# First layer's norm: adaLN weights in groups of 256 channels, each chunk normed, modulated and multiplied as its group arrives

## The chip, the cores and the metric

One core of a Trainium2 chip runs the whole kernel. The metric is device time in microseconds (us). Engines are named as in the profile: PE (TensorE, matrix products), PEld (its weight loads), DVE (VectorE), ACT (ScalarE), POOL (GpSimd), SP (SyncE, which issues most of the DMA transfers).

## The reference, cut to what matters

Two layers run one after the other on a residual stream x of 1024 tokens by 1024 channels. Each layer norms and modulates its input, projects it to 5912 columns, runs two attention mixers and adds a gated output projection:

```
mod = silu(c) @ ada_w + ada_b                 # c: 1024 values; ada_w: 1024 x 3072 per layer
shift, scale, gate = split(mod, 3)
h = rms_norm(x, norm_g) * (1 + scale) + shift
proj = h @ w_in                               # 1024 x 5912
a = stick_breaking_attention(sb_q, sb_k, sb_v) * silu(sb_z)
b = native_sparse_attention(rope(rms_norm(n_q)), ...) * silu(n_z)
y = sigmoid(m_a) * (a @ w_proj_a) + sigmoid(m_b) * (b @ w_proj_b)
x = x + gate * (y @ w_out)
```

All is float32. The change touches the first three lines, and the first product of the fourth, in layer 0 alone.

## The kernel before

A float32 product runs as three passes: each operand is split into a high part (rounded on ACT, `hi`) and a low part (difference on DVE, `lo`), and hi*hi, hi*lo and lo*hi are summed in PSUM. Channels are handled in 8 chunks of 128, tokens in 2 halves of 512. The normed input is held transposed, channels on partitions, so that scale and shift are one number per partition: `A = norm_g * (1 + scale)` and `B = shift`, as [128, 8] columns.

The function `norm_first` is the start of the kernel. PE, DVE and ACT run its instructions in the order in which it writes them (`manual_schedule`, L326); what later functions emit is placed between them by the planner of the framework. SP issues loads in the order written, and a load into a buffer that is still in use makes SP, and all loads behind it, wait.

In order, `norm_first` does this:

- SP loads four x tiles (first half, 512 KB each, L465), the identity (L519) and three small vectors (c, ada_b, norm_g; L341 to L343), then the scale part of ada_w as 8 tiles [128, 1024] through 5 buffers (L472), three raw weight tiles of the first projection group (L175), the shift part of ada_w in the same way, the fourth raw tile and the four x tiles of the second half. The rope tables, the masks and the next group's weights follow.
- ACT squares the x tiles (L488). DVE turns the vectors into columns (L347) and makes silu(c) (L350).
- `rsqrt` takes three Newton steps on a [128, 4] tile: start value on DVE (L146 to L148), 12 steps on POOL (L152 to L155), since `on_pool` is set here. ACT then scales the x tiles (L529), PE transposes them (L436), and ACT copies all 8 transposed chunks out of PSUM (L532).
- DVE sums the scale part over the 8 tiles, `acc = acc + ada * silu(c)_k` (L478, L481); PE multiplies each 128-column slice of `acc` with a column of ones (L373), which sums over partitions; DVE makes A (L540, L541). The shift part goes the same way and gives B in two halves of 4 chunks (L546).
- `chunks(0, ...)`: for each chunk `modulate` makes `h = x*A + B` and its high part on ACT (L444, L445, even chunks) or h on DVE and the high part on ACT (L447, L448, odd chunks), then the low part on DVE (L449); then 6 products per chunk (L496), for two column groups of 128 by three passes. Between them, on ACT and DVE, lie squares (L488, L490), Newton steps and scaling of the second half, and the splits of the weight tiles (L136, L137).
- `chunks(1, ...)` does the same for the second half, with the transposes (L436) between the products and the rope tables (L635) on DVE. The low part of a chunk is taken after the next chunk's first step.

The results of the first half lie in two PSUM buffers (`proj`), those of the second in two others (`sc`). Then `early` goes on with the other projection groups (lines L194, L196, L198 in the profile); they need the split weights and a `proj` buffer.

Of the kernel before, what the change touches and what calls it, by code (L numbers as in the profile page):

```python
# [37 lines left out]
def make_consts():  # L38
    """Constants that depend on shapes alone, packed along the free dimension of 128 partitions."""
# [48 lines left out]
class Trunk:  # L88
    def __init__(self, tc, I, O, depth=2, dbg=None):
# [7 lines left out]
        # amount of projection work that is put between the bursts of an attention job, by query pair  # L97
# [5 lines left out]
        # how far dependent transposes are put off  # L103
# [9 lines left out]
        self.adb = 5  # L113

    # ---------------------------------------------------------------- helpers
# [23 lines left out]
    def rsqrt(self, pool, ss, n, inv, tag, on_pool=False):  # L139
        """1/sqrt(ss * inv + EPS) by Newton steps; ss [rows, n]."""  # L140
# [9 lines left out]
        for _ in range(3):  # L150
            if on_pool:
                nc.gpsimd.tensor_tensor(t, y, y, ALU.mult)  # L152
                nc.gpsimd.tensor_tensor(t, t, v, ALU.mult)
                nc.gpsimd.tensor_scalar(t, t, -0.5, 1.5, ALU.mult, ALU.add)
                nc.gpsimd.tensor_tensor(y, y, t, ALU.mult)  # L155
            else:
                nc.vector.tensor_tensor(t, y, y, ALU.mult)
                nc.vector.scalar_tensor_tensor(t, t, -0.5, v, ALU.mult, ALU.mult)
                nc.vector.scalar_tensor_tensor(y, t, 1.5, y, ALU.add, ALU.mult)
# [18 lines left out]
    def split_raw(self, raw):  # L178
        """Tile [128, hi/lo, 2, columns]."""
        n = raw.shape[2]  # L180
        w = self.tl(self.wpool, [P, 2, 2, 280], F32R, "w", bufs=self.wb)
        self.split(raw, w[:, 0, :, :n], w[:, 1, :, :n])
        return w

    def load_group(self, srcs, ncols):
        """The four tiles of a weight group."""
        return [self.split_raw(raw) for raw in self.load_raw(srcs, ncols)]

    def mm3_gen(self, ps, pairs, cost):
        """Three-pass product over pairs ((lhs_hi, lhs_lo), (rhs_hi, rhs_lo)), matmul by matmul."""  # L190
# [21 lines left out]
    def t_unit(self, w, u, half, act, ks=range(KD)):  # L212
        """[128 columns, 512 tokens] = w columns^T @ act^T for one half of the tokens."""
# [4 lines left out]
    def n_unit(self, w, t, act, ncols):  # L218
        """[128 tokens, ncols] = act tokens @ w."""
# [4 lines left out]
    def n_units(self, w, ts, act, ncols):  # L224
        """n_unit of several token tiles, the last chunk of the contraction after the others of all."""
# [16 lines left out]
    def defer(self, us, f):  # L242
        """Emit f once us of tensor-engine work have gone by, so that its operands are ready."""
# [58 lines left out]
    # ---------------------------------------------------------------- start  # L302
# [30 lines left out]
    # ---------------------------------------------------------------- adaLN modulation  # L333
    def vectors(self, pool, l):
        """Biases of the modulation [128, shift/scale, 8] and norm gain [128, 8] of layer l, model dimension on
        partitions; the first layer's call also makes silu(c)."""
        nc, I = self.nc, self.I
        n = 32 if l == 0 else 24
        rows = self.tl(pool, [n, P], F32, "vrows")
        if l == 0:  # L340
            nc.sync.dma_start(rows[24:32], I["c"].rearrange("o (k p) -> (o k) p", p=P))  # L341
        nc.sync.dma_start(rows[0:16], I["ada_b"][l, 0:2 * D].rearrange("(k p) -> k p", p=P))
        nc.sync.dma_start(rows[16:24], I["norm_g"][l].rearrange("(k p) -> k p", p=P))  # L343
# [9 lines left out]
    def mod_part(self, pool, l, part, sc, tag, steps):  # L353
        """acc[p, j] = sum over chunks k of ada_w[k*128+p, part*1024 + j] * silu(c)[k*128+p], one step per chunk."""
# [45 lines left out]
    def mod_gate(self, l, pool, steps):  # L400
        """The residual gate on every partition; returns it and the part that uses the tensor engine."""
# [13 lines left out]
    # ---------------------------------------------------------------- norm  # L415
# [4 lines left out]
    def norm_rows(self, pool, xs, tag, on_pool=False):  # L420
        """x * rsqrt(mean(x^2) + eps), in place, of the [128, 1024] tiles xs."""
# [6 lines left out]
        r = self.rsqrt(pool, ss, n, 1.0 / D, tag, on_pool)  # L428
# [3 lines left out]
    def norm_t(self, xs, k):  # L432
        """PSUM [128 channels of chunk k, 512 tokens]."""
# [5 lines left out]
    def modulate(self, pool, src, a, b, hi, lo, bufs=2, on_scalar=False):  # L439
        """src * a + b, split; returns the last step."""  # L440
# [10 lines left out]
    def norm_first(self):  # L451
        """Norm of the input, and the first product on it, in the order in which the loads arrive."""
        tc, nc, I = self.tc, self.nc, self.I
        rope = self.open_rope(0)
        with tc.tile_pool(name="norm0", bufs=1, reuse_waits="tile") as pool:
            A = self.tl(self.lay, [P, KD], F32, "Acol", bufs=2)
            B = self.tl(self.lay, [P, KD], F32, "Bcol", bufs=2)
            ada = {}
            acc = [self.tl(pool, [P, D], F32, f"acc{part}") for part in range(2)]

            def load_x(half):
                xs = []
                for t in range(4):
                    x = self.tl(pool, [P, D], F32, "x", bufs=4)
# [4 lines left out]
            def load_ada(part):  # L469
                for k in range(KD):  # L470
                    a = self.tl(pool, [P, D], F32, "ada", bufs=self.adb)
# [981 lines left out]
```

## Time and profile before

| | |
|---|---|
| median of 3 runs | 2231.28 us (2230.01 to 2231.57) |
| span of the profiled execution | 2229.4 us |
| PE busy | 2131.1 us, 96% |
| DVE busy | 1572.0 us, 71% |
| ACT busy | 1129.2 us, 51% |
| POOL busy | 60.2 us, 3% |
| mean granted PE clock | 0.992 |

The execution's own time is its span from first to last instruction; the runs' times hold a little more around it. A granted clock of 1.00 is 2.4 GHz, 0.50 is 1.2 GHz. Busy shares are averages over the whole kernel; a stretch is read from the tables by stretch, and a chain of waits shows which wait ended last.

### The profile page before, as it was taken

What the parts mean: (1) busy time and instruction counts of PE and PEld (TensorE: products, weight loads), DVE (VectorE), ACT (ScalarE), POOL (GpSimd) and SP (SyncE); (2) the same over time, 40 slices, a digit from 0 to 9 for tenths busy, and PEclk for the clock granted to TensorE, in tenths of its full rate; (3) what the DMA queues carried; (4) which work ended last, traced back from release to release, by engine and by line L of the source; (5) the groups of instructions that cost most, each with busy time, mean ns of one, the idle gap of its engine ahead of it and who ended that gap; (6) DMA issues with size and microseconds to landing.
All of it is one profiled execution on the core that took longest, in us unless ns stands there. A gap on an engine that the chain in (4) does not pass through costs nothing.

```text
span 2229.4 us, 36753 instructions
## 1 busy us (share of the span) xinstructions
PE 2131.1 (96%) x13128; PEld 1841.4 (83%) x13128; DVE 1572.0 (71%) x3714; ACT 1129.2 (51%) x2481; POOL 60.2 (3%) x226
## 2 busy tenths in 40 slices
PE   3999999999999999999999998999999999999999
PEld 3899778988887777789889986889898877777899
DVE  5857558868765877877765852887788487787643
ACT  4533147656665655663443421665666465656410
POOL 2100000000000000000010000000000000001000
PEclk8999999999999999999999999999999999999999
DMA  7435862252116445275455355322522364534433
GB/s 286 131 124 180 250 156 79 88 151 96 66 49 165 127 125 137 86 246 174 159 149 160 97 189 141 94 86 86 142 91 67 92 154 112 149 100 168 150 123 102
DMA packets 239256, 297.04 MB, mean 133 GB/s; under 512 B 21993, under 2 KB 186721, under 8 KB 239073
## 3 DMA queue, kind: packets, MB, share of 16 engines
q1 hardware_dynamic: 198560, 250.65, 36.6%
q10 hardware_dynamic: 36224, 29.37, 5.1%
q0 software_dynamic: 4288, 14.68, 2.0%
q8 instruction: 103, 1.69, 0.3%
q14 instruction: 81, 0.66, 0.1%
HBM read 206.28 MB, written 83.89 MB: 130 GB/s over the span
## 4 chain that ended last, share of the span: by engine, by line
PE 66%; DVE 17%; DMA 7%; issue 5%; ACT 3%; POOL 1%; SPq 0%; ACTq 0%; DVEq 0%; POOLq 0%
PE proj L194 15%; PE proj L198 15%; PE proj L196 15%; PE tr L879 6%; DVE C L1243 4%; PE av L899 4%; PE av L898 3%; PE sc L866 3%; PE sc L867 3%; DVE wl L137 2%; DVE E L1244 2%; DMA ada<-in_ada_w 2%; DVE w L137 2%; DMA kk<-QK 1%; DMA q<-QK 1%
## 5 line engine op out<-in xcount | busy, mean ns | idle before, releaser
L194 PE MATMUL proj<-acthi,w 128*128 128x512 f32 x1312 | 536.9, 409 | 1.3 <-ACT acthi L136 0.7
L196 PE MATMUL proj<-actlo,w 128*128 128x512 f32 x1312 | 536.8, 409 | 0.5 <-DVE actlo L137 0.5
L198 PE MATMUL proj<-acthi,w 128*128 128x512 f32 x1312 | 536.2, 409 | 0.7 <-DVE w L137 0.7
L136 ACT CAST w<-raw 128x512 fp32r<-128x512 f32 (+1 forms) x296 | 183.4, 622 | 230.1 <-PE proj L198 119.0
L137 DVE TENSOR_TENSOR wl<-tr,wh 128x512 fp32r<-128x512 f32 (+2 forms) x432 | 256.6, 610 | 40.8 <-ACT wh L136 38.4
L194 PEld LDWEIGHTS proj<-acthi,w 128*128 128x128 f32 x1312 | 249.4, 190 | 42.1 <-ACT acthi L136 1.6
L196 PEld LDWEIGHTS proj<-actlo,w 128*128 128x128 f32 x1312 | 249.4, 190 | 39.0 <-DVE actlo L137 1.9
L198 PEld LDWEIGHTS proj<-acthi,w 128*128 128x128 f32 x1312 | 249.0, 190 | 37.9 <-DVE w L137 1.2
L137 DVE TENSOR_TENSOR w<-raw,w 128x512 fp32r<-128x512 f32 (+1 forms) x296 | 202.2, 688 | 81.9 <-ACT w L136 79.8
L136 ACT CAST wh<-tr 128x512 fp32r<-128x512 f32 (+2 forms) x432 | 221.2, 527 | 76.1 <-PE tr L879 70.7
L899 PE MATMUL av<-wl,V 128*128 128x256 f32 (+1 forms) x864 | 217.5, 285 | 7.6 <-DVE wl L137 7.3
L194 PE MATMUL proj<-w,acthi 128*128 128x256 f32 (+1 forms) x768 | 221.2, 288 | 2.2 <-DVE s L137 1.7
L198 PE MATMUL proj<-w,actlo 128*128 128x256 f32 (+1 forms) x768 | 221.0, 288 | 0.0
L196 PE MATMUL proj<-w,acthi 128*128 128x256 f32 (+1 forms) x768 | 219.8, 286 | 0.0
L898 PE MATMUL av<-wh,V 128*128 128x256 f32 (+1 forms) x864 | 216.8, 271 | 1.2 <-DVE o L917 0.5
L879 PE MATMUL tr<-ident,E 128*128 128x128 f32 x1152 | 187.3, 276 | 23.7 <-DVE E L1244 23.0
L1243 DVE TENSOR_TENSOR_SCAN C<-C 128x128 f32<-128x128 f32 (+7 forms) x128 | 172.5, 1349 | 53.0 <-ACT C L1239 52.4
L879 PEld LDWEIGHTS tr<-ident,E 128*128 128x128 f32 x1152 | 139.2, 140 | 67.4 <-DVE E L1244 35.0
L899 PEld LDWEIGHTS av<-wl,V 128*128 128x128 f32 x864 | 162.7, 188 | 31.1 <-DVE wl L137 19.3
L866 PE MATMUL sc<-kk,q 128*128 128x512 f32 (+3 forms) x512 | 176.8, 346 | 8.6 <-DVE mx L1079 4.1
L867 PE MATMUL sc<-kk,q 128*128 128x512 f32 (+3 forms) x512 | 175.5, 343 | 0.0
L898 PEld LDWEIGHTS av<-wh,V 128*128 128x128 f32 x864 | 163.0, 189 | 14.0 <-ACT wh L136 3.9
(247 smaller groups left out, 3898.2 us busy)
## 6 DMA issues: line engine op xcount, KB each, us to landing
raw<-in_w_in SPq DMA_DIRECT2D x168, 256.0 KB, 2.9
ada<-in_ada_w SPq DMA_DIRECT2D x48, 512.0 KB, 5.3
kk<-QK SPq DMA_DIRECT2D x48, 512.0 KB, 9.0
q<-QK ACTq DMA_DIRECT2D x64, 256.0 KB, 4.0
QK<-s SPq DMA_DIRECT2D x32, 512.0 KB, 3.0
MD<-sz SPq DMA_DIRECT2D x64, 256.0 KB, 2.6
QK<-s SPq DMA_DIRECT2D x48, 256.0 KB, 3.3
VD<-s SPq DMA_DIRECT2D x48, 256.0 KB, 2.1
```

The source lines that it names most:

```text
L136: nc.scalar.copy(hi, src)
L137: nc.vector.tensor_tensor(lo, src, hi.bitcast(F32), ALU.subtract)
L194: nc.tensor.matmul(ps, lh, rh, start=(x == 0), stop=False)
L196: nc.tensor.matmul(ps, lh, rl, start=False, stop=False)
L198: nc.tensor.matmul(ps, ll, rh, start=False, stop=(x == n - 1))
L866: nc.tensor.matmul(ps, q, k[:, 0, c0:c1], start=True, stop=False)
L867: nc.tensor.matmul(ps, q, k[:, 1, c0:c1], start=False, stop=not masks)
L879: nc.tensor.transpose(pt[:, x * P:x * P + P], b, self.ident)
L898: nc.tensor.matmul(ps[:, c:d], lhsT, hi[:, a:b], start=(first and x == 0), stop=False, skip_group_check=True)
L899: nc.tensor.matmul(ps[:, c:d], lhsT, lo[:, a:b], start=False, stop=(last and x == n - 1), skip_group_check=True)
L1243: nc.vector.tensor_tensor_scan(rev, rev, rev, 1.0, ALU.mult, ALU.bypass)
L1244: nc.vector.tensor_tensor(e[:, 0:nk], e[:, 0:nk], c[:, 1:nk + 1], ALU.mult)
```

## The change

`rsqrt` loses `on_pool`; all its steps run on DVE (3 per Newton step instead of 4). The identity and the three small vectors are issued by ACT instead of SP. ada_w's scale and shift parts come in 4 groups of 256 channels each, one tile [128, 8, 256] per part and group, by two DMAs of 512 KB whose rows are 1 KB; three such buffers serve both parts. The x tiles have 8 buffers instead of 4.

The scale part of a group is now summed on PE: 8 accumulating products of a 128 x 128 block with a column of silu(c), for each of 2 chunks. The shift part is summed on DVE over 256 columns and then over partitions on PE. The copies of the transposed chunks are gone; `modulate` reads PSUM. All 8 chunks of the first half use the form with h and high part on ACT, and the low part is taken at once, in both halves. Squares, Newton steps and scaling of the second half follow the last chunk of the first half; squares alternate between ACT and DVE, and so does scaling, in both halves.

The core of the diff (old `load_ada`, `add`, `chunks` and the old sequence are removed):

```diff
-            if on_pool:
-                nc.gpsimd.tensor_tensor(t, y, y, ALU.mult)
-                ...
-            else:
-                nc.vector.tensor_tensor(t, y, y, ALU.mult)
+            nc.vector.tensor_tensor(t, y, y, ALU.mult)
...
+            def load_ada(part, g):
+                a = self.tl(pool, [P, KD, W], F32, "ada", bufs=3)
+                src = I["ada_w"][0, :, part * D + g * W:part * D + g * W + W].rearrange("(k p) n -> p k n", p=P)
+                for k in range(0, KD, 4):
+                    nc.sync.dma_start(a[:, k:k + 4], src[:, k:k + 4])
+                return a
...
+            def scale_cols(g):
+                a = ada[1, g]
+                pt = self.tl(self.pav, [P, 512], F32, "av", bufs=1)
+                for j in range(2):
+                    for k in range(KD):
+                        nc.tensor.matmul(pt[:, j:j + 1], a[:, k, j * P:j * P + P], sc[:, k:k + 1],
+                                         start=(k == 0), stop=(k == KD - 1))
+                return pt
+            def shift_acc(g):
+                a = ada[0, g]
+                acc = self.tl(pool, [P, W], F32, "acc", bufs=2)
+                nc.vector.tensor_scalar(acc, a[:, 0], sc[:, 0:1], None, ALU.mult)
+                for k in range(1, KD):
+                    nc.vector.scalar_tensor_tensor(acc, a[:, k], sc[:, k:k + 1], acc, ALU.mult, ALU.add)
+                return acc
+            def shift_cols(acc):      # two products of acc with ones, in a "tr" buffer of PSUM
...
+            xs = [load_x(0)]
+            ab, gn = self.vectors(pool, 0, nc.scalar)
...
+            for part in (1, 0):
+                ada[part, 0] = load_ada(part, 0)
+            gen = self.plan.pop(0)()
+            raws = [next(gen) for _ in range(2)]
             for t in range(4):
+                square(0, t, t % 2 == 0)
+            r = self.rsqrt(pool, ss[0], 4, 1.0 / D, "nr0")
+            for t in range(4):
+                scale(0, t, r)
+            w = [self.split_raw(raws[0])]
+            for g in range(1, G):
+                for part in (1, 0):
+                    ada[part, g] = load_ada(part, g)
+                if g < 3:
+                    raws.append(next(gen))
             xs.append(load_x(1))
+            tr = [self.norm_t(xs[0], 0), self.norm_t(xs[0], 1)]
+            pa = scale_cols(0)
+            fin_a(0, pa)
+            fin_b(0, shift_cols(shift_acc(0)))
+            for g in range(G):
+                k = 2 * g
+                mod(0, k, tr.pop(0), True)
+                if g + 1 < G:
+                    pa = scale_cols(g + 1)
+                mm(0, k)
+                mod(0, k + 1, tr.pop(0), True)
+                if g + 1 < G:
+                    tr.append(self.norm_t(xs[0], k + 2))
+                    w.append(self.split_raw(raws[g + 1]))
+                    fin_a(g + 1, pa)
+                    acc = shift_acc(g + 1)
+                mm(0, k + 1)
+                if g + 1 < G:
+                    tr.append(self.norm_t(xs[0], k + 3))
+                    fin_b(g + 1, shift_cols(acc))
+            for t in range(4):
+                square(1, t, t % 2 == 0)
+            r = self.rsqrt(pool, ss[1], 4, 1.0 / D, "nr1")
+            for t in range(4):
+                scale(1, t, r)
             tables = rope()
             next(tables)
+            for k in range(KD):
+                mod(1, k, self.norm_t(xs[1], k), k % 2 == 0)
+                if k:
+                    mm(1, k - 1)
+                next(tables, None)
+            mm(1, KD - 1)
```

## Rows read from the trace of the kernel before

**Rows 1.** The page's second part, 40 equal slices: PE's busy tenths.
```profile
PE   3999999999999999999999998999999999999999
```
**Rows 2.** Stretches: bounds, length, busy us (instructions) per engine, granted clock, DMA share, GB/s.
```profile
33.00:42.00 9.00, 1.67 (x15) 1.59 (x15) 7.11 (x9) 1.70 (x4) 0.00 (x0) 0.65 0.53 187
46.00:56.00 10.00, 8.96 (x19) 6.24 (x20) 8.80 (x19) 9.20 (x15) 1.55 (x4) 0.50 0.53 155
56.00:63.00 7.00, 6.86 (x29) 5.22 (x28) 4.66 (x11) 4.39 (x7) 2.04 (x9) 0.99 0.00 0
84.00:110.00 26.00, 26.00 (x211) 25.57 (x210) 24.57 (x106) 10.44 (x25) 4.27 (x8) 1.00 0.81 228
291.50:295.00 3.50, 3.50 (x17) 3.49 (x18) 0.64 (x4) 0.00 (x0) 0.00 (x0) 0.52 1.11 350
```
**Rows 3.** Chain that ended last, first 80 us: start, us, what.
```profile
3.94 6.27 DMA vrows<-in_norm_g
...
12.65 1.17 POOL nr0t L152
...
22.82 4.28 ACT x L529 x4
27.14 5.85 PE tr L436 x29
...
44.25 0.17 DVE Bcol L546
```
**Rows 4.** Groups by line and shape, first 110 us: busy, mean ns; idle before.
```profile
L481 DVE SCALAR_TENSOR_TENSOR acc<-ada,silu_c,acc 128x1024 f32<-128x1024 f32 x12 | 15.4, 1284 | 0.9 <-DMA ada<-in_ada_w 0.6
L449 DVE TENSOR_TENSOR actlo<-h,acthi 128x512 fp32r<-128x512 f32 x16 | 10.8, 682 | 0.0
L445 ACT CAST acthi<-h 128x512 fp32r<-128x512 f32 x8 | 5.0, 620 | 0.3
L444 ACT ACTIVATE h<-xt,Bcol,Acol 128x512 f32<-128x512 f32 x4 | 3.2, 809 | 10.5 <-DVE Bcol L546 9.8 <-DVE actlo L449 0.7
L481 DVE SCALAR_TENSOR_TENSOR acc<-ada,silu_c,acc 128x512 f32<-128x512 f32 x4 | 2.8, 750 | 0.7 <-DMA ada<-in_ada_w 0.7
L490 DVE CUSTOM_DVE_ANT_0 junk<-x 128x1024 bf16<-128x1024 f32 x2 | 2.4, 1217 | 0.0
```
**Rows 5.** Instructions in order of time: start, us, engine, line, operation.
```profile
9.54 1.06 ACT L488 ACTIVATE junk<-x 128x1024 bf16<-128x1024 f32 x1 [0.15 <-DMA x<-in_x]
...
53.55 0.17 DVE L146 TENSOR_SCALAR nr1v<-ss 128x4 f32<-128x4 f32 x1
53.75 0.17 DVE L147 TENSOR_SCALAR nr1i<-nr1v 128x4 int32<-128x4 int32 x1
...
63.26 1.03 PE L436 MATMUL tr<-ident,x 128*128 128x128 f32 x8
```
**Rows 6.** Instructions in order of time: products of one column on PE.
```profile
32.83 1.84 PE L373 MATMUL av<-ones,acc 128*128 128x1 f32 x16
...
42.38 1.84 PE L373 MATMUL tr<-ones,acc 128*128 128x1 f32 x8 [7.70 <-DVE acc L481]
...
289.65 5.00 PE L373 MATMUL proj<-ones,acc 128*128 128x1 f32 x32
```
**Rows 7.** Instructions in order of time: products of the first half.
```profile
51.35 1.05 PE L496 MATMUL proj<-acthi,w 128*128 128x512 f32 x2
...
52.63 1.05 PE L496 MATMUL proj<-acthi,w 128*128 128x512 f32 x2
```
**Rows 8.** Stretches, columns as in rows 2, with loads of 1 KB rows.
```profile
17.00:19.00 2.00, 0.00 (x0) 0.00 (x0) 1.96 (x2) 0.00 (x0) 1.92 (x2) 1.00 0.79 221
...
998.00:1000.00 2.00, 1.94 (x16) 1.97 (x17) 1.81 (x3) 0.31 (x1) 0.00 (x0) 1.00 0.96 315
```
**Rows 9.** Line 669, 80 to 95 us: POOL's copies into xs; landing holds SP's too.
```profile
L669 POOL DMA_DIRECT2D xs<-s x8: 598/598/808, 83.1 to 92.9; - x8
...
DMA to landing us min/median/max: 2.4/4.1/5.5
```

More of the change, by code (lines that the diff above doesn't have):

```diff
@@ L331, in run, with vectors @@
                 xsrc = dst
-    def vectors(self, pool, l):
+    def vectors(self, pool, l, eng=None):
         nc, I = self.nc, self.I
+        eng = eng or nc.sync
         n = 32 if l == 0 else 24
@@ L457, in norm_first @@
             B = self.tl(self.lay, [P, KD], F32, "Bcol", bufs=2)
-            ada = {}
-            acc = [self.tl(pool, [P, D], F32, f"acc{part}") for part in range(2)]
+            warm = self.tl(pool, [P, 1], F32, "warm")
+            nc.scalar.activation(warm, self.ones[:, 0:1], AF.Sigmoid)
+            nc.scalar.dma_start(self.ident, I["consts"][:, 0:P])
             def load_x(half):
@@ L467, in load_x, with square @@
                 return xs
-            def load_ada(part):
-                for k in range(KD):
-                    a = self.tl(pool, [P, D], F32, "ada", bufs=self.adb)
-                    nc.sync.dma_start(a, I["ada_w"][0, k * P:(k + 1) * P, part * D:part * D + D])
-                    ada[part, k] = a
-            def add(part, k0, k1):
-                for k in range(k0, k1):
-                    if k == 0:
-                        nc.vector.tensor_scalar(acc[part], ada[part, k], sc[:, 0:1], None, ALU.mult)
-                        continue
-                    for c in (slice(0, 512), slice(512, 1024)) if k == KD - 1 else (slice(0, 1024),):
-                        nc.vector.scalar_tensor_tensor(acc[part][:, c], ada[part, k][:, c], sc[:, k:k + 1],
-                                                       acc[part][:, c], ALU.mult, ALU.add)
-            def square(half, t, on_scalar=True):
+            def load_ada(part, g):
[4 more added lines that the diff above has]
+                return a
+            def square(half, t, on_scalar):
                 junk = self.tl(pool, [P, D], BF16, "junk")
@@ L490, in square, with scale @@
                     nc.vector.tensor_tensor_reduce(junk, xs[half][t], xs[half][t], 1.0, 0.0, ALU.mult, ALU.add, s)
+            def scale(half, t, r):
+                if t % 2:
+                    nc.scalar.mul(xs[half][t], xs[half][t], r[:, t:t + 1])
+                else:
+                    nc.vector.tensor_scalar(xs[half][t], xs[half][t], r[:, t:t + 1], None, ALU.mult)
             def mm(half, k):
@@ L497, in mm @@
                                          start=(k == 0 and x == 0), stop=(k == KD - 1 and x == 2))
-            def chunks(half, src, between):
-                hi, lo = act[half]
-                fin = None
-                for k in range(KD):
-                    f = self.modulate(pool, src(k), A[:, k:k + 1], B[:, k:k + 1], hi[:, k], lo[:, k], 3, k % 2 == 0)
-                    if fin:
-                        fin()
-                        mm(half, k - 1)
-                    fin = f
-                    for g in between.get(k, []):
-                        g()
-                fin()
-                mm(half, KD - 1)
@@ new lines, in shift_acc @@
+            def shift_acc(g):
[6 more added lines that the diff above has]
+            def shift_cols(acc):
+                pt = self.tl(self.ptr, [P, 512], F32, "tr", bufs=self.trb)
+                for j in range(2):
+                    nc.tensor.matmul(pt[:, j:j + 1], acc[:, j * P:j * P + P], self.ones[:, 0:1], start=True, stop=True)
+                return pt
@@ new lines, in fin_a, with fin_b, mod @@
+            def fin_a(g, pt):
+                k = slice(2 * g, 2 * g + 2)
+                nc.vector.scalar_tensor_tensor(A[:, k], pt[:, 0:2], 1.0, ab[:, 1, k], ALU.add, ALU.add)
+                nc.vector.tensor_tensor(A[:, k], A[:, k], gn[:, k], ALU.mult)
+            def fin_b(g, pt):
+                k = slice(2 * g, 2 * g + 2)
+                nc.vector.tensor_tensor(B[:, k], pt[:, 0:2], ab[:, 0, k], ALU.add)
+            def mod(half, k, src, on_scalar):
+                hi, lo = act[half]
+                self.modulate(pool, src, A[:, k:k + 1], B[:, k:k + 1], hi[:, k], lo[:, k], 3, on_scalar)()
@@ L515, in norm_first @@
             xs = [load_x(0)]
             ss = [self.tl(pool, [P, 4], F32, f"ss{h}") for h in range(2)]
-            for t in range(4):
-                square(0, t)
-            nc.sync.dma_start(self.ident, I["consts"][:, 0:P])
-            ab, gn = self.vectors(pool, 0)
+            ab, gn = self.vectors(pool, 0, nc.scalar)
             sc = self.sc
@@ L535, in norm_first @@
-            gen = self.plan.pop(0)()
-            raws = [next(gen) for _ in range(3)]
-            load_ada(0)
-            raws.append(next(gen))
-            add(0, 0, 3)
-            nc.vector.scalar_tensor_tensor(A, p1, 1.0, ab[:, 1], ALU.add, ALU.add)
-            nc.vector.tensor_tensor(A, A, gn, ALU.mult)
-            w = [self.split_raw(x) for x in raws[:2]]
-            add(0, 3, KD)
-            for h in range(0, KD, 4):
-                pb = self.mod_cols(acc[0], self.pav if h else self.ptr, "av" if h else "tr", 1 if h else self.trb, h, h + 4)
-                nc.vector.tensor_tensor(B[:, h:h + 4], pb[:, h:h + 4], ab[:, 0, h:h + 4], ALU.add)
@@ L547, in norm_first @@
[L547 to L566 removed]
+            ada = {}
@@ L567, in norm_first @@
+            for t in range(4):
[3 more added lines that the diff above has]
+                scale(1, t, r)
             tables = rope()
             next(tables)
-            chunks(1, lambda k: self.norm_t(xs[1], k), {k: [lambda: next(tables, None)] for k in range(8)})
+            for k in range(KD):
[3 more added lines that the diff above has]
+                next(tables, None)
```

49 lines of the change are left out of this document (10 added, 39 removed).

## The prediction

> **What bounds the kernel now.** I read the page's 40 slices first, then a table of stretches, then the chain of waits, and then single durations. The slices show the PE full in all but the first one [rows 1], so a change to the first norm can only move what happens before the PE is full for good. The stretches put that point at 56 us: the PE is busy 6.86 of the 7 us from 56 to 63, and after 84 us it has no gap [rows 2]. From there everything later shifts as one block, so what counts is when the PE has done the same work as in the kernel before.
>
> My mark is the end of the first four transposes of the second half of the tokens, its chunk 0. Eight start at 63.26 and take 1.03 [rows 5], so four are done at 63.8, directly behind the last product of the first half, and the PE is then at 2.4 GHz (granted clock 0.99 in 56:63, 1.00 in 84:110 [rows 2]). Up to there the chain of waits goes: small vectors landing at 10.2, Newton steps on POOL from 12.7 to 22.8, scaling on ACT, transposes, the sums of both modulation parts on DVE, and B ready at 44.4 [rows 3]. The products of the first half then run from 46 to 63, for ten of these seventeen us at a granted clock of 0.50 [rows 2]. At 1.2 GHz three products take 1.28 us, 0.427 each [rows 7]; in 56:63 they take 0.237.
>
> **The change: the first B.** The fourth x tile still lands at 9.5, since its square starts then [rows 5]. Its square on DVE takes 1.2 [rows 4], to 10.7. Newton is 12 DVE instructions 0.20 apart [rows 5], 2.4 us, to 13.1; on POOL it took 10.2 [rows 3]. Two scalings on ACT at 4.28/4 = 1.07 [rows 3] end at 15.3. The last transposes of chunk 0 and the four of chunk 1 cost 5 x 0.20 (5.85/29 [rows 3]) = 1.0, to 16.4. Then come 16 one-column products for the scale: 1.84/16 = 0.115 each at 2.4 GHz, 1.84/8 = 0.23 at 1.2 GHz [rows 6]. The PE has done little before, and in the kernel before the transposes from 27 us on ran at 0.20 against 0.13 at 63 us [rows 3, 5], so I take 1.2 GHz: 3.7, to 20.1 (1.9 less otherwise). A needs two small DVE steps, 0.4. The shift sums: on 1024 columns an add takes 1.28, on 512 it takes 0.72 to 0.75 [rows 4]; continued to 256 columns that is about 0.42 (0.48 at most), 8 x 0.42 = 3.4. Two one-column products with hand-over 0.7, the add 0.2, small hand-overs 0.2: first B at 25.0 instead of 44.3 for its first half.
>
> What could delay this is the identity and the small vectors, which move to ACT's queue. Now SP has issued them by 3.9, and they land at 10.2 behind x on the same queue [rows 3]. The nearest row of a second queue beside a busy one is the copies into xs, 128 KB in 2.4 to 5.5 us [rows 9]. Issued by about 4 as now, they land by 8 in the middle of that, and the fourth x tile remains the last. Bounds: no loss, or 3.2 us if they still come at 10.3, since sigmoid and silu stand ahead of the squares on ACT and DVE. The four issues on ACT themselves stand only ahead of that sigmoid. The Trainium skill, "DMA: Bandwidth & Descriptors", Queues, rings and completion order, says that each engine takes turns between the queues that have work; by it the loss is 0. The section Issuing engines are not separate DMA queues says that a second issuer saves only issue time; by that alone it would be the 3.2. No row of these very loads on ACT's queue decides.
>
> **Part 2: the groups.** B of one group to B of the next is a chain, since each engine keeps the written order. By ACT and DVE: two times h 0.81 and its rounding 0.62 plus a weight rounding of the same 0.62, together 3.5; the weight's low part 0.7; A 0.4; shift sums 3.4; two products, hand-over and add 0.9; sum 8.9 [rows 4, 6]. By the PE at 1.2 GHz: 16 x 0.23 + 12 x 0.427 + 8 x 0.20 + 0.8 = 3.7 + 5.1 + 1.6 + 0.8 = 11.2 [rows 3, 6, 7]. At 2.4 GHz the PE needs 1.8 + 2.8 + 1.0 + 0.6 = 6.2 and ACT and DVE set the pace. So a group costs 8.9 to 11.2. One-column products don't hold the clock: 32 of them from 289.65 on kept the PE busy [rows 6], and the granted clock is 0.52 in 291.5:295 [rows 2]. But each group also holds products and transposes without a gap, 5.1 + 1.6 = 6.7 at 1.2 GHz, and such stretches did raise the clock: the transposes from 27.1 took 0.20 each, and behind them 0.115 per one-column product means 2.4 GHz [rows 3, 6]; 46:56 is at 0.50, 56:63 at 0.99 [rows 2]. For the first group I take the middle, 10.0; a later one may start while the clock is still up, 9.0 each. Sum 28 (26.7 to 33.6), so the last B is at 53.0.
>
> The loads stay ahead of this. Their rows are 1 KB: such rows moved at 221 GB/s for the first weights (17:19, share 0.79) and at 315 in 998:1000, share 0.96 [rows 8]. At 315, 1.05 MB takes 3.3. Three buffers make SP wait, with the raw weights, the x tiles of the second half, the rope tables and the mask constants queued behind. The last shift load is issued when the third group's scale products end, near 38, and lands near 43; its sums start near B of the third group + 4.5 = 48.5. The second half's x follows and lands near 49, wanted at 56. At 221 GB/s a load takes 4.7 and the last lands near 51: 2.7 late. I take 0.
>
> **Part 3: the second half.** Its squares, Newton and scaling, which now lie beside the first half's products, come after the last chunk. From the last B: low part of chunk 7 at +3.7, two DVE squares 2.4, Newton 2.4, two ACT scalings 2.2, transpose 0.3: +11.0, so 64.0 against 63.8. From first B to mark it was 63.8 - 44.4 = 19.4 and becomes 28 + 11 = 39; the 19.4 won on the first B are given back. What is late next is this very chain: the first half's products end at about +6.5, 59.5, and the PE has some 3 us without work before the first scaled x tile.
>
> After the mark the work on the PE is as before, 8 x (6 products + 4 transposes), with products of the next weight group in its gaps. Two differences. After the idle 3 us I expect the clock at 1.2 GHz (it fell to 0.65 on average in 33:42, and PE was idle for most of that [rows 2]); at 1.2 GHz half the time is lost: nothing if it is up, 5 if it stays down for ten us as in 46:56, and I take the middle, 2.5. And the low part is now taken at once, so DVE waits 0.6 to 0.8 for each rounding in four odd chunks; most lies under the PE's own work, I take 0.7 (0 to 2.5). Against this, the next group's first 24 products could fill the idle stretch, 0 to 2.8; they need DVE steps while DVE is the busy engine, so I take 0. Gone at no cost: eight ACT copies of the transposed half, half of the DVE sums, all beside other work or inside the stage. Total: 0.2 + 2.5 + 0.7 = +3.4.
>
> **Sum.** The profiled span of 2229.4 becomes 2232.8. The median of the runs, 2231.3, is 1.9 above the span, what lies around it, and I let that stay: 2234.7.
>
> **Rivals.**
> Slower by the clock: PE at 1.2 GHz sets all three groups at 11.2, so 33.6 instead of 28: +5.6 on the forecast, 2240.3. For it: the one-column products and waits split each group, and 46:56 at clock 0.50 shows ten us of nearly full PE without a rise [rows 2]. Against: the unbroken 6.7 us. It decides from a mean group of 9.7 on (1.1 more in all reaches the bound for slower, below). Chance 0.25. The Trainium skill, "TensorE: Matmul & The Clock Gate", HAM oscillation, tells of loops whose bursts are parted by waits and which start every burst at the low clock; by it this is the likely case. The trace agrees for 46:56, and not for 56:63.
>
> Slower by the loads: vectors at 10.3 (+3.2, 2237.9) or 1 KB rows at 221 GB/s (+2.7, 2237.4). Chance 0.13; each reaches past the bound.
>
> Faster: the clock is up in the groups, or their unbroken stretch lifts it early. Then B starts 1.9 earlier, groups are 8.9 (26.7), the mark is at 60.8 and the 2.5 at entry are gone: -3.0 + 0.7, and with the gap filled by the next group's products (2.8) -5.1: 2226.2. For it: B 19 us earlier, and transposes and products side by side. Against: 32 one-column products at 289 us. Chance 0.16.
>
> That the change does not do what it says: the second half's chain would have to move up, which the written order forbids; its gain is then only the one above.
>
> **Numbers.** Forecast 0.46, own range 2229 to 2236 (below: no loss behind the mark and the idle stretch filled; above: the bound to slower). 0.2% is 4.5 us, about what a measurement here tells from no change. Faster 0.16 (the faster rival), slower 0.38 (the two slower ones), within 0.46. Range 2226 to 2241: the faster rival's end just in, each slower rival in, two of them together out.
>
> **What would show it.** POOL has no Newton rows; the Newton rows on DVE span 2.4. Four Bcol rows, the first at 25, the others 9 to 10 apart, the last near 53. Granted clock at 0.5 for most of 15 to 55. The second half's squares only after the last chunk's low part, first transposes of it ending at 64, PE idle for some 3 us before them. Wrong if the Bcol rows are under 8.5 or over 10.5 apart on average, if the groups wait on ada loads, if vcols is copied at 10 us, or if the PE works on the next weight group (lines 194 to 198) before 62.

## The result

The changed kernel takes 2250.14 us (median of four runs, 2244.68 to 2250.9) where the kernel before takes 2231.43 beside it: ratio 1.0078, 95% interval 1.0066 to 1.0091. It is slower by some 18.7 us. The forecast was 2234.7, and the time lies outside the range, above it. The profiled span is 2249.1, 16.3 above the forecast span of 2232.8.

The page of the changed kernel, its second part (40 slices), PE's busy tenths and the granted clock, answers to [rows 1]:

```profile
PE   6899999999999999999999999899999999999999
PEclk9899999999999999999999999999999999999999
```

The first slice is fuller than before, since PE now works in it, and the second is no longer full. Of the 19.7 us that the span has grown, 16.3 are there when these slices are over (the same DVE instructions of both kernels compared at 150 us).

Stretches of the changed kernel, columns as in [rows 2]:

```profile
30.13:63.61 33.48, 33.47 (x172) 30.39 (x172) 18.28 (x42) 9.64 (x15) 0.00 (x0) 0.85 0.81 269
33.00:42.00 9.00, 9.00 (x38) 8.18 (x38) 5.53 (x13) 1.62 (x3) 0.00 (x0) 1.00 0.49 164
46.00:56.00 10.00, 10.00 (x59) 9.01 (x58) 6.31 (x15) 3.97 (x7) 0.00 (x0) 0.75 0.97 343
56.00:63.00 7.00, 7.00 (x29) 6.00 (x29) 5.00 (x12) 0.21 (x1) 0.00 (x0) 0.62 0.89 261
63.00:84.00 21.00, 14.40 (x64) 10.21 (x63) 13.95 (x36) 12.26 (x19) 0.00 (x0) 0.87 0.14 38
84.00:110.00 26.00, 25.29 (x165) 22.23 (x164) 20.91 (x68) 12.63 (x24) 7.03 (x13) 0.98 0.41 104
```

From 30.1 to 63.6 us PE has no free time at all, where I had expected ACT and DVE to set the pace; and from 63 to 84, where the kernel before kept it busy for 20.16 of 21 us, it is busy for 14.4. The granted clock of 1.00 in 33:42 can't be taken at its word: the first change that the trace records is at 40.8, and up to there the column shows 1.00, although the 32 instructions of L501 (below) take 6.8 us before it and 3.6 behind it.

The chain that ended last in the changed kernel, its first 100 us (start, us, what), answers to [rows 3]:

```profile
2.11 5.31 DMA vrows<-in_ada_b
...
11.94 1.23 DVE junk L480
...
15.59 2.20 ACT x L484 x2
17.83 1.33 PE tr L430 x5
19.16 6.63 PE av L501 x32
...
30.13 1.01 PE tr L516 x4
31.14 6.83 PE av L501 x32
37.97 2.77 PE proj L492 x6
40.74 0.54 PE tr L430 x4
41.28 1.40 PE proj L492 x6
42.67 0.44 PE tr L430 x4
43.11 0.34 PE tr L516 x4
43.45 3.57 PE av L501 x32
...
52.70 5.10 PE av L501 x32
...
69.43 1.28 DVE w L136 x2
70.71 1.14 DVE junk L480
71.86 0.60 DVE s L136
...
77.36 0.79 ACT h L438
```

This is the heart of the case. L501 holds the 16 one-column products of a group, and each group shows 32 of them: **a float32 product is two instructions on PE.** (The products of the rounded halves, L492, and the transposes, L430, show one each: x6 and x4.) They cost 6.63, 6.83, 3.57 and 5.10 us, 22.1 in all, in a chain in which I had 3.7 for a group. DVE and ACT in order of time (start, us, engine, line, what, and in brackets the wait) show what hangs on them:

```profile
9.49 1.23 DVE L480 CUSTOM_DVE_ANT_0 junk<-x 128x1024 bf16<-128x1024 f32 x1 [0.87 <-ACT junk L478]
...
10.75 1.06 ACT L478 ACTIVATE junk<-x 128x1024 bf16<-128x1024 f32 x1 [1.30 <-DVE ss L480]
...
11.94 1.23 DVE L480 CUSTOM_DVE_ANT_0 junk<-x 128x1024 bf16<-128x1024 f32 x1 [1.22 <-ACT junk L478]
...
25.81 0.16 DVE L521 SCALAR_TENSOR_TENSOR Acol<-av,vcols 128x2 f32<-128x2 f32 x1 [6.80 <-PE av L501]
...
26.46 3.61 DVE L510 SCALAR_TENSOR_TENSOR acc<-ada,silu_c,acc 128x256 f32<-128x256 f32 x7
31.18 0.16 DVE L526 TENSOR_TENSOR Bcol<-tr,vcols 128x2 f32<-128x2 f32 x1 [1.10 <-PE tr L516]
...
38.66 3.61 DVE L510 SCALAR_TENSOR_TENSOR acc<-ada,silu_c,acc 128x256 f32<-128x256 f32 x7
...
43.49 0.16 DVE L526 TENSOR_TENSOR Bcol<-tr,vcols 128x2 f32<-128x2 f32 x1 [1.22 <-PE tr L516]
...
52.73 0.16 DVE L526 TENSOR_TENSOR Bcol<-tr,vcols 128x2 f32<-128x2 f32 x1 [0.80 <-PE tr L516]
...
63.63 0.16 DVE L526 TENSOR_TENSOR Bcol<-tr,vcols 128x2 f32<-128x2 f32 x1 [1.54 <-PE tr L516]
```

The first three are the squares, to which I come back. At 25.81 DVE has stood 6.80 us for the scale products; it makes A, and only then sums the shift part. So in front of the first B the two ways of summing run one after the other.

Between the Bs it is otherwise: there the chain is PE alone, without a stop. The shift sums that start at 38.66 are done at 42.27, and PE comes to their two products (L516) only at 43.11; in the next two groups it comes 0.4 and 1.2 us after the sums. B comes at 31.2, 43.5, 52.7 and 63.6. The groups are 12.3, 9.2 and 10.9 long; the 32 instructions in them take 6.83, 3.57 and 5.10, and what is left, 5.5, 5.7 and 5.8, is PE's other work: 12 products of h, 8 transposes and the two products of the shift part. PE sets the groups, and how long its work takes follows the clock.

As the mark I now use the start of the first h of the second half on ACT, right behind the transposes that the prediction marked: 63.9 in the kernel before, 77.4 here. Against the forecast of 64.0 the loss is +6.2 to the first B, +4.4 in the groups and +2.7 from the last B on. The other 3.0 of the 16.3 by which the span exceeds the forecast span come much later, and are left open below.

### The profile page after: what moved, and what is told of

It reads as the page before. It is cut to its first block, busy times and chain, and to the rows that moved or that the text cites. A ratio compares the mean times of both kernels' runs of the same rounds, so it can differ in the third digit from the quotient of the medians.

```text
span 2249.1 us, 36960 instructions
## 1 busy us (share of the span) xinstructions
PE 2154.6 (96%) x13240; PEld 1863.4 (83%) x13240; DVE 1575.7 (70%) x3756; ACT 1123.7 (50%) x2471; POOL 47.1 (2%) x202
## 4 chain that ended last, share of the span: by engine, by line
PE 68%; DVE 17%; DMA 8%; ACT 3%; issue 3%; SPq 0%; ACTq 0%; DVEq 0%; POOL 0%; POOLq 0%
PE proj L187 15%; PE proj L191 15%; PE proj L189 15%; PE tr L898 5%; DVE C L1262 4%; PE av L918 3%; PE av L917 3%; PE sc L885 3%; PE sc L886 3%; DVE wl L136 3%; DVE E L1263 2%; DMA ada<-in_ada_w 2%; DVE w L136 2%; DMA q<-QK 1%; PE av L501 1%
## 5 line engine op out<-in xcount | busy, mean ns | idle before, releaser
L136 DVE TENSOR_TENSOR wl<-tr,wh 128x512 fp32r<-128x512 f32 (+2 forms) x432 | 257.0, 611 | 41.4 <-ACT wh L135 39.0
L136 DVE TENSOR_TENSOR w<-raw,w 128x512 fp32r<-128x512 f32 (+1 forms) x296 | 202.7, 689 | 84.3 <-ACT w L135 80.8
L898 PEld LDWEIGHTS tr<-ident,E 128*128 128x128 f32 x1152 | 139.1, 140 | 67.3 <-DVE E L1263 35.3
L917 PEld LDWEIGHTS av<-wh,V 128*128 128x128 f32 x864 | 163.1, 189 | 13.8 <-ACT wh L135 3.6
```

The source lines that it names most:

```text
L898: nc.tensor.transpose(pt[:, x * P:x * P + P], b, self.ident)
L917: nc.tensor.matmul(ps[:, c:d], lhsT, hi[:, a:b], start=(first and x == 0), stop=False, skip_group_check=True)
```

## The experiments

Theory A: the one-column products, at two instructions each, are the term that went wrong, first by their own time and second because A and the shift sums stand behind them. Theory B: the half clock is what costs, and the products don't matter. Other suspects: the squares, which take turns, and the second half's chain. Ratios are against the kernel before on the same chip, with 95% intervals; the mark and the Bs are from the profiled execution. The kernel before had a median of 2233.49 beside e1 to e4, 2232.12 beside e5 to e7 and r_after, and 2235.95 beside e8 to e10, so medians of different sets are compared by their ratios.

The time follows the mark only roughly. Against the changed kernel e2_junk2 has its mark 1.8 earlier and a profiled span 6.8 shorter, e5_shift_first its mark 1.8 earlier and a span 0.8 longer. So the argument rests on the Bs and the mark, and the times give its direction.

| kernel | first B | groups | mark | median us | ratio |
|---|---|---|---|---|---|
| before | 44.3 | - | 63.9 | 2231.43 | 1 |
| changed | 31.2 | 12.3, 9.2, 10.9 | 77.4 | 2250.14 | 1.0078 [1.0066, 1.0091] |
| changed, again (r_after) | 31.2 | 13.2, 10.9, 9.3 | 79.7 | 2249.61 | 1.0078 [1.0065, 1.0091] |
| e1_scale_one | 25.0 | 9.2, 9.2, 9.2 | 67.6 | 2237.17 | 1.0015 [1.0006, 1.0025] |
| e2_junk2 | 29.5 | 13.0, 9.2, 10.9 | 75.6 | 2244.37 | 1.0043 [1.0031, 1.0055] |
| e3_half1_early | 31.1 | 12.8, 9.3, 10.9 | 71.7 | 2243.90 | 1.0044 [1.0030, 1.0058] |
| e4_before_newton_dve | 37.3 | - | 57.1 | 2228.91 | 0.9984 [0.9974, 0.9994] |
| e5_shift_first | 26.8 | 13.4, 10.9, 9.3 | 75.6 | 2244.65 | 1.0053 [1.0037, 1.0069] |
| e6_group_best | 24.5 | 13.8, 10.9, 10.9 | 67.3 | 2237.79 | 1.0025 [1.0015, 1.0034] |
| e7_before_best | 34.8 | - | 56.2 | 2224.18 | 0.9966 [0.9953, 0.9979] |
| e8_warm | 34.2 | - | 56.0 | 2221.44 | 0.9945 [0.9930, 0.9959] |
| e9_pool_scale | 27.0 | 18.1, 14.0, 18.8 | 86.1 | 2255.83 | 1.0101 [1.0084, 1.0117] |
| e10_group_one | 22.0 | 8.9, 8.9, 9.1 | 56.2 | 2225.57 | 0.9960 [0.9945, 0.9974] |

**Fewer scale products.**

```diff
 def scale_cols(g):
-    for k in range(KD):
+    for k in range(1):
         ...
-                         start=(k == 0), stop=(k == KD - 1))
+                         start=True, stop=True)
```

> Leaves out 7 of the 8 terms of each scale column: 2 one-column products per group stand where 16 stood. Theory A (the one-column products, two TensorE instructions each, are what my sum mis-sized): the first B comes 6 us earlier (25 instead of 31.2), the groups take 9.0 to 10.0 each instead of 12.3, 9.2 and 10.9, and the mark (first transposes of the second half, 77.4 in the changed kernel) falls to 66 to 68: 2238 to 2241 in all. Theory B (the half clock, which few columns bring about, and not the products themselves): with still fewer columns before the first B the clock stays low as long; the first B moves by 2 to 3 at most and the groups stay above 10.5: 2246 to 2250. Theory C (the loads set the groups): no change at all, 2250.

Four instructions a group remain. DVE in order of time, the Bs:

```profile
25.04 0.16 DVE L526 TENSOR_TENSOR Bcol<-tr,vcols 128x2 f32<-128x2 f32 x1 [1.11 <-PE tr L516]
...
34.20 0.16 DVE L526 TENSOR_TENSOR Bcol<-tr,vcols 128x2 f32<-128x2 f32 x1 [0.70 <-PE tr L516]
...
52.50 0.16 DVE L526 TENSOR_TENSOR Bcol<-tr,vcols 128x2 f32<-128x2 f32 x1 [0.70 <-PE tr L516]
```

Theory A: first B 6.2 earlier, groups 9.2, mark 67.6; the median, 2237.17, is 0.8 under what it gave. Stretches of this kernel (columns as above) answer theory B:

```profile
33.00:42.00 9.00, 6.84 (x28) 5.25 (x28) 5.91 (x14) 3.22 (x5) 0.00 (x0) 0.81 0.86 294
42.00:52.00 10.00, 8.03 (x30) 6.12 (x30) 6.65 (x16) 3.21 (x5) 0.00 (x0) 0.66 0.94 305
```

The clock is at 0.66 in 42:52, where the changed kernel was granted 0.83, and yet the groups are shorter and even. With the products gone PE has time over in two of the three groups, and the clock no longer sets their pace. In the last group, at half clock from 44.2 to 51.0, there is nothing to spare: PE is done with its transposes at 51.87 and DVE with its sums at 51.80.

**Two buffers for the squares.**

```diff
-    junk = self.tl(pool, [P, D], BF16, "junk")
+    junk = self.tl(pool, [P, D], BF16, "junk", bufs=2)
```

> Two buffers instead of one for the squares' discarded output. Theory A (one buffer makes the squares of ScalarE and VectorE take turns): both engines square at once, r is there at 13.1 instead of 15.6, and the second half's r 2.4 earlier as well; the first B doesn't move (TensorE's scale products set it), so the mark falls by 2.4 and the time to 2246 to 2248. Rival (the four sums share one tile, and that is what orders them, or the scalings are ordered behind the loads): nothing moves, 2250.

In the changed kernel the squares of the first half take turns, each waiting for the other engine's (9.49 to 11.94 above). With two buffers, the same view, they lie side by side:

```profile
8.89 1.22 DVE L480 CUSTOM_DVE_ANT_0 junk<-x 128x1024 bf16<-128x1024 f32 x1
...
9.85 1.06 ACT L478 ACTIVATE junk<-x 128x1024 bf16<-128x1024 f32 x1
...
10.15 1.23 DVE L480 CUSTOM_DVE_ANT_0 junk<-x 128x1024 bf16<-128x1024 f32 x1
```

So the buffer orders them, not the tile of sums. r comes 1.7 earlier (13.9, not 15.6), and so does the first B, which I had said would stay: the whole first chain hangs on r. The mark moves by 1.8, theory A's 2.4 nearly, but not for its reason: from the last B to the mark it is 13.1 in place of 13.7, so the second buffer gives only 0.6 in the second half. The median, 2244.37, is lower than theory A's 2246 to 2248, by more than the mark explains.

**The second half's norm earlier.**

```diff
 for g in range(G):
     ...
+    if g == 3:
+        r = self.rsqrt(pool, ss[1], 4, 1.0 / D, "nr1")
     mod(0, k + 1, tr.pop(0), True)
     ...
+    if g == 2:
+        for t in range(4):
+            square(1, t, True)
     mm(0, k + 1)
-for t in range(4):
-    square(1, t, t % 2 == 0)
-r = self.rsqrt(pool, ss[1], 4, 1.0 / D, "nr1")
```

> The second half's squares (all four on ScalarE) stand in the third group and its Newton steps in the fourth, instead of both behind the last chunk; the scalings stay behind it. Theory A (the second half's chain behind the last chunk costs its whole length): the mark falls by 6 (4.9 of squares, some 2 of Newton, less 1 that the four squares cost ScalarE inside the groups): 2243 to 2245. Rival (ScalarE, which makes both h and hi, sets the groups): four squares of 1.2 push the fourth group by 4.9, the mark falls by 1 to 2 only: 2248 to 2249.

The mark falls by 5.7, as theory A had it, and the groups hardly change: ACT has room for four squares.

**Newton steps alone.**

```diff
-r = self.rsqrt(pool, ss[0], 4, 1.0 / D, "nr0", True)
+r = self.rsqrt(pool, ss[0], 4, 1.0 / D, "nr0")
-    nr[1] = self.rsqrt(pool, ss[1], 4, 1.0 / D, "nr1", True)
+    nr[1] = self.rsqrt(pool, ss[1], 4, 1.0 / D, "nr1")
```

> The kernel before with its Newton steps on VectorE and nothing else changed. Theory A (in the kernel before, the first norm is not what its first h waits for: the modulation's sums are): within 2 us, 2230 to 2233. Rival (POOL's Newton steps are on the path in both halves, and taking them off gives their length back): 8 us faster, 2222 to 2224; then the other parts of the change together cost 27 and not 19.

The rival's mechanism, with about half its size in the time: B 7.0 earlier, the mark 6.8, and the median 4.6 below that of the kernel before (3.6 by the ratio, 1.3 to 5.8). So this one part of the change is good, and the rest of it costs some 21 (by the ratios) to 23 us (18.7 + 4.6), not 19.

**Shift sums ahead of A.**

```diff
-fin_a(0, pa)
-fin_b(0, shift_cols(shift_acc(0)))
+acc = shift_acc(0)
+fin_a(0, pa)
+fin_b(0, shift_cols(acc))
 ...
-    fin_a(g + 1, pa)
     acc = shift_acc(g + 1)
+    fin_a(g + 1, pa)
```

> The changed kernel with each group's shift sums emitted ahead of the step that makes A, on VectorE; nothing else. In the changed kernel VectorE stands 6.80 us on the scale products and only then begins 4.0 us of shift sums. Theory A (the two ways of summing run one after the other only because A stands ahead of the sums on VectorE): the sums lie beside the scale products, the first B comes 4 earlier (27 instead of 31.2), the later groups lose 0 to 3 each (TensorE's own 7.0 at 1.2 GHz, 3.7 at 2.4, remain), the mark falls by 4 to 9 to 68 to 73: 2241 to 2246. Rival (TensorE's sum of work sets the groups, whatever VectorE does): the first B gains 4, the later groups get longer by as much, the mark stays within 2 of 77.4.

The first B gains 4.4 and the groups none: 13.4, 10.9, 9.3. DVE, the second and third B, and PE's stretch between them:

```profile
40.23 0.16 DVE L526 TENSOR_TENSOR Bcol<-tr,vcols 128x2 f32<-128x2 f32 x1 [4.97 <-PE tr L516]
...
51.10 0.16 DVE L526 TENSOR_TENSOR Bcol<-tr,vcols 128x2 f32<-128x2 f32 x1 [2.42 <-PE tr L516]
```

```profile
24.00:33.00 9.00, 9.00 (x43) 9.00 (x44) 4.24 (x11) 3.21 (x5) 0.00 (x0) 1.00 0.68 219
33.00:42.00 9.00, 9.00 (x45) 7.79 (x45) 2.39 (x8) 1.54 (x3) 0.00 (x0) 1.00 0.93 302
```

Theory A held for the first B; for the groups the rival did, as the changed kernel's own chain, PE alone between the Bs, lets one expect. DVE's wait for PE at the second B grows from 1.22 to 4.97, and PE is as full as it was. So the products cost in two ways: in front of the first B they hold up DVE, and in the groups they and PE's other work fill PE. The mark, 75.6, stands against 77.4 and 79.7 of the same groups with A first. The median, 2244.65, lies in theory A's range all the same, and the six runs spread from 2240.55 to 2252.08: the time does not decide here, the Bs do.

**All repairs together** (shift first, two buffers, second half early).

> The changed kernel with shift sums first, two junk buffers, and the second half's squares and Newton steps inside the third and fourth group. If the three repairs add (1.8 and 5.7 measured for two of them, 4 to 9 expected for the third), the mark is at 61 to 66 and the time within 4 of the kernel before, that is 2230 to 2236 beside a kernel before of 2232. Rival (they overlap, since ScalarE's four squares and the earlier start leave TensorE at 1.2 GHz): mark 67 to 70, 2237 to 2241.

The first B is at 24.5, the groups 13.8, 10.9 and 10.9, the mark 67.3, the time 2237.79: the rival's. The repairs in front of the first B are in part lost in the groups, where PE is the bound.

**The same, with one scale term** (the edits of e6_group_best and e1_scale_one).

> The repaired changed kernel, leaving out 7 of the 8 terms of each scale column. If the one-column products set its groups (TensorE), they fall to 7 to 8.5, below the 9.2 of the single removal since the shift sums now stand first; first B at 21 to 22, mark 52 to 55: 2222 to 2227. Rival (the clock, or ScalarE with h, hi and squares): groups stay at 9 or above, mark 57 or later, 2228 to 2231.

Neither had it right: the groups are 8.9, 8.9 and 9.1, the mark 56.2. With PE relieved the first two come to rest on ACT and DVE, which the prediction had added up to 8.9, so theory A's 7 to 8.5 was too low. That the sums agree to the tenth is chance: in this chain neither A nor a weight's rounding lies, a chunk's low part does (0.6), and the shift sums take 3.9 and not 3.4. The last group, at half clock from 41.0 to 47.8, ends on PE. Against e6_group_best the products alone are worth 11.1 of the mark and, in ratio, 0.65% of the time.

**Scale sums on POOL.**

```diff
 def scale_cols(g):
-    for j in range(2):
-        for k in range(KD):
-            nc.tensor.matmul(pt[:, j:j + 1], a[:, k, j * P:j * P + P], sc[:, k:k + 1], ...)
+    nc.gpsimd.tensor_scalar(acc, a[:, 0], sc[:, 0:1], None, ALU.mult)
+    for k in range(1, KD):
+        nc.gpsimd.tensor_scalar(a[:, k], a[:, k], sc[:, k:k + 1], None, ALU.mult)
+        nc.gpsimd.tensor_tensor(acc, acc, a[:, k], ALU.add)
```

The rest is that of e6_group_best; `acc` is then summed over partitions by two products with ones on PE, and the shift sums have one buffer instead of two.

> The repaired changed kernel (shift sums first, two junk buffers, second half's squares and Newton steps early) with the scale sums taken from TensorE and put on POOL, as multiply and add on 256 columns, 15 instructions a group. If POOL does a pair in under 1.1 (a group's sum in 9), the groups fall from 13.8, 10.8, 10.9 to about 9 and the mark from 67 to 58 to 61: 2227 to 2231. Rival (POOL is slower than that, or slows VectorE): groups of 12 or more, 2238 or later.

The rival. Groups of POOL by line and shape, 10 to 80 us (columns as in [rows 4]):

```profile
L501 POOL TENSOR_SCALAR ada<-ada,silu_c 128x256 f32<-128x256 f32 x28 | 27.5, 988 | 3.8 <-DMA ada<-in_ada_w 3.8
L502 POOL TENSOR_TENSOR acg<-acg,ada 128x256 f32<-128x256 f32 x28 | 24.5, 876 | 0.7
```

A pair takes 1.86, a group's seven pairs 13.0; the groups become 14.0 to 18.8. Ahead of its last sum POOL also stood 3.57 us for a load of ada (from 54.36 on), so the last group is not POOL's arithmetic alone.

**The kernel before, reordered.**

```diff
 # Newton steps on VectorE, as in e4
-raws = [next(gen) for _ in range(3)]
 load_ada(0)
-raws.append(next(gen))
+raws = [next(gen) for _ in range(4)]
 ...
-w = [self.split_raw(x) for x in raws[:2]]
 add(0, 3, KD)
+w = [self.split_raw(x) for x in raws[:2]]
```

> The kernel before with the Newton steps on VectorE, the first weights loaded behind the shift half of the modulation weights instead of ahead of it, and their two roundings behind the sums. With the Newton steps alone B was at 37.3, and VectorE had 2.2 us of waits for loads and 1.3 of weight roundings ahead of it. Theory A (loads and VectorE are both at their limit up to B): B at 34 to 35, mark 3 earlier, 4 to 7 faster than the kernel before: 2225 to 2228 beside 2232. Rival (the weights now land too late for the first products, or the lower clock eats it): B at 34 to 35 but the mark unmoved at 57, 2229.

B comes 2.5 earlier than with the Newton steps alone and the mark only 0.9: the mark is the rival's, the time a little better than theory A's (2224.18, 7.9 less than the kernel before). This kernel beats both that the case began with.

**PE kept busy for a part of its wait for B** (40 transposes more in e7_before_best, output unread).

```diff
+for x in range(10):
+    self.norm_t(xs[0], x % KD)
 gen = self.plan.pop(0)()
```

> The reordered kernel before (Newton on VectorE, weights behind the modulation loads), with 40 transposes more on TensorE, whose output nobody reads, in the 11 us in which it waits for B. Theory (what the first half's products lose there is the half clock that follows TensorE's idle stretch): the clock is up when B comes, B itself comes 1 to 2 earlier (its one-column products at half their time), the first products lie nearer together and the mark moves from 56 to 52 to 54: 2220 to 2222. Rival (VectorE and ScalarE set the first half's chunks, as their rows of 4 to 5 us a pair suggest): B 1 to 2 earlier, mark the same or 1 earlier, 2223 to 2224.

The mark is the rival's, with B only 0.6 earlier. Stretches of e7_before_best:

```profile
22.00:34.00 12.00, 3.42 (x28) 3.33 (x26) 11.11 (x13) 2.59 (x5) 0.00 (x0) 0.74 1.00 375
34.00:44.00 10.00, 8.87 (x29) 6.46 (x30) 7.31 (x14) 8.65 (x15) 0.00 (x0) 0.63 0.87 287
```

and of this kernel:

```profile
22.00:34.00 12.00, 9.06 (x75) 8.85 (x74) 11.18 (x14) 2.91 (x5) 0.00 (x0) 0.97 1.00 385
34.00:44.00 10.00, 8.26 (x26) 5.58 (x26) 6.99 (x14) 8.57 (x14) 0.00 (x0) 0.70 0.77 258
```

But the theory is not tested by this: its condition, the clock up when B comes, was not met. PE of this kernel in order of time:

```profile
25.04 4.56 PE L436 MATMUL tr<-ident,x 128*128 128x128 f32 x40
32.54 1.21 PE L373 MATMUL tr<-ones,acc 128*128 128x1 f32 x8 [2.94 <-DVE acc L481]
```

The 40 transposes end at 29.6, PE stands 2.94 us for the last shift sum, and the granted clock is 0.50 from 33.2 to 40.1. B comes at 34.2, and the first products of h run at half clock, as in e7_before_best (half from 27.8 to 41.4). ACT is busy for 8.65 and 8.57 of 10 us in 34:44. The mark moves by 0.2; what a clock that is up at B would be worth stays open. The median is lower than e7_before_best's, but the intervals of the two ratios overlap, so that it is faster than that one is not shown.

**The changed kernel again.**

> The changed kernel itself, for comparison on the same chip: 2244 to 2251, mark at 77.4.

The first B is the same to 0.1, the groups come in another order (13.2, 10.9, 9.3), and the mark is 2.3 later than expected, 79.7. PE is alone on the chain between the Bs here too, and the clock's first rise is at 42.8 and not at 40.8: the lengths follow where the clock's changes fall, which differs from one execution to the next.

## Why the prediction was wrong, step by step

**The step that failed** is "16 one-column products ... 1.84/16 = 0.115 each at 2.4 GHz, 1.84/8 = 0.23 at 1.2 GHz [rows 6]". Its rows count instructions, and I took them for products. The row of 16 is eight columns of one product each, the row of 8 four columns; both are two instructions a product, which the code named beside them (eight and four columns) would have told. A product is 0.23 at 2.4 GHz and 0.43 at 1.2 (6.83/16). So the 3.7 is 6.83. It entered in three places:
- First B: +3.1 of the 6.2.
- The groups: I had one chain of ACT and DVE (8.9) and one of PE, 11.2 at 1.2 GHz and 6.2 at 2.4, and let a group lie between 8.9 and 11.2. With 6.83 and 3.57 for its first term PE's sum is 14.3 and 8.0. So PE, not ACT and DVE, set all three groups, at a clock that was down for part of the time: 12.3, 9.2 and 10.9, where I had 10.0, 9.0 and 9.0.
- The rival "slower by the clock", in which PE sets the groups, had its price, 11.2 a group, from the same count. Its mechanism is the one that the chain shows, and the mean group, 10.8, is above its deciding point of 9.7 and above the 10.5 that I had named as a sign of being wrong; its 2240.3 was still 10 short.

That this is the term is shown by e1_scale_one: without those products the first B is at 25.0, the groups are 9.2 (forecast 10.0, 9.0, 9.0) and the last B is at 52.5 (forecast 53.0). That its first B meets the forecast is chance, though: the run leaves out some 6 us of products where the forecast counts 3.7 for them, and the next two steps make up the difference.

**A second step, smaller:** "Its square on DVE takes 1.2 [rows 4], to 10.7" and "two DVE squares 2.4" supposed that ACT and DVE square side by side. One buffer makes them take turns: Newton begins at 13.2 and not at 10.7. That is +2.5 ahead of the first B. A second buffer gives back 1.7; the other 0.8 is that even then the squares begin only at 8.7, behind what is done with the vectors on both engines. Behind the last B the +2.7 are 0.6 from the buffer and 1.9 from low parts of operands of the next stage, which DVE makes between and behind the squares (L136 in the chain of the changed kernel: 1.28 at 69.43 and 0.60 at 71.86); I had counted the second half's chain as if DVE had nothing else. In the same stretch PE did some of the next group's products (14.4 us busy in 63:84), for which I had taken 0.

**A third:** the adds on 256 columns follow each other every 0.52 (3.61/7), not 0.42: +0.6 in front of the first B. The line through 1.28 on 1024 columns and 0.75 on 512 gives 0.48 at 256, which I had put down as the most; one add does take 0.48, and the 0.03 from one to the next was left out.

**What held.** Newton on DVE takes 2.4, POOL has none. The vectors land at 7.4 (the chain's 2.11 + 5.31), not 10.2 [rows 3]: the 3.2 that I had as a bound are not lost; the squares, which stand behind the vectors, begin 0.8 late, as said. The rule of the Trainium skill, "DMA: Bandwidth & Descriptors", Queues, rings and completion order, that the engines take turns between queues, agrees with these 7.4. No group waits for a load; in 46:56, with 1 KB rows and rows of x side by side, 343 GB/s were moved, above the 315 of [rows 8]. The second half's chain is where I put it, and costs its length: e3_half1_early takes 5.7 of it away. Behind the mark the clock is down from 78.4 to 85.2; at 150 us the kernel is 16.3 late, 2.9 more than at the mark, for 3.2 forecast.

The clock goes up and down in the changed kernel, seven changes from 40.8 to 85.2. The Trainium skill, "TensorE: Matmul & The Clock Gate", HAM oscillation, tells of this for bursts that are parted by waits. The trace agrees with the ups and downs, not with the waits: PE had none before the falls at 47.7 and 54.5. The first came behind 32 one-column instructions (43.45 to 47.02), the second amid the next 32 (from 52.70). In e1_scale_one the clock was low for as long (10 us between the first rise and the last B in both) and the groups are an even 9.2. So the half clock cost time where PE set the groups, and the miscounted products had made it do so.

**Left open.** At 310 us the changed kernel is 22.3 behind the kernel before (same DVE instructions compared) and at 250 only 17.4; at the end it is 19.7. In the profile PE waits there 3.55 us for a load of q, and the granted clock falls at the end of that wait (324.1). The profile of the kernel before has no such wait; all the others have it, from 0.4 to 3.6 us, those without groups too. Runs of one kernel differ by more (e5_shift_first 2240.55 to 2252.08). What sets this wait is not shown; no run tried it.

## What to carry to other kernels

Before a row's time is divided by its count, settle what one count is: here one float32 product is two instructions, and the loop that issues them says how many products there should be. When a reduction is moved to an engine, follow the chain through both engines in the written order, not each engine's sum alone: in front of the first B the cheap sums on DVE stood behind a wait for PE, and in the groups PE was full, so that moving them ahead gained nothing there. And try the parts of a change alone: the Newton steps on DVE gained 4.6 us by themselves (3.6 by the ratio), inside a change that lost 18.7. Before a run is read as a test of a theory, see in its trace that the theory's condition was met: in e8_warm PE stood idle again before B came.

## What the runs showed of the hardware

- A one-column float32 product on PE shows as two instructions, of 0.115 each at 2.4 GHz and 0.21 at 1.2: 0.23 and 0.43 a product for 128 numbers out.
- On POOL a multiply of 128x256 float32 takes 0.99 and an add 0.88, 1.86 a pair; on DVE one instruction does both, 0.52 from one to the next.
- Up to the first change on record the granted clock reads 1.00 even where the clock is down: in the changed kernel 32 instructions take 6.83 under that reading, and 3.57 after it rose.
- The granted clock fell with PE busy without a stop (33.47 of 33.48 us in 30.13:63.61 of the changed kernel): at 47.7 behind 32 one-column instructions and at 54.5 amid the next 32.
